# Selections ahead of the sliding part, early output norms, ten half-sequence tiles, and pair sums on VectorE

## The chip, the cores and the metric

The kernel runs on one core of a Trainium2 chip. The metric is the device time of one launch in microseconds (us); where several runs are told of, their median is meant. Engines are called PE (TensorE), DVE (VectorE), ACT (ScalarE), POOL (GpSimd) and SP (SyncE, which issues DMAs).

## The reference, cut to what matters

The program is one inference step of one decoder layer, for one prompt of 512 tokens and for eight sample sequences of 4 new tokens with 2048 past tokens each. Both share the weights and go through the same steps:

```
h = rmsnorm(x);  P = h @ W_in
x += W_out [ headnorm(NSA(P)) || sigmoid(o) * headnorm(mLSTM(P)) ]
x += CrossAttn(rmsnorm(x), memory);  x += SwiGLU(rmsnorm(x))
```

NSA is an attention in three branches per key-value group g (two groups). The compressed branch attends to 127 compressed blocks per sequence; they come from `compress`, run once for keys and once for values:

```
first = ch @ w1[:half];  second = ch @ w1[half:]      # ch: 16 tokens of one head side by side
hid = first + shift(second) + (pe @ w1 + b1);  out = gelu(hid) @ w2
```

The selected branch scores 64-token blocks by the compressed branch's probabilities, keeps the best 16, and attends to their raw rows:

```
imp = cmp_to_sel(p_c.sum(2));  imp = where(forced, 1e9, imp)
_, idx = top_k(imp, 16);       k_sel = gather(ks, idx); v_sel = gather(vs, idx)
```

The third branch is a sliding window of 512 tokens. Each head's output is then normalised.

## The kernel before

Products in fp32 are made of three matmuls in a reduced fp32 format: `split` (L212) writes a high part on ACT (L213) and the rest on DVE or POOL (L214), and `mm3` (L216) issues high by high, high by low, low by high (L218 to L220 in the trace).

The stages follow one another: the input projection, the prompt's attention and mLSTM, `compress(0)` for the keys, `compress(1)` for the values, the output projection w_out, cross attention, the feed-forward part. `weave` (L315) puts two streams of work into one program: `compress` is the background and pays 0.6 per yield, and the foreground (L1812) is the chain of prompt work, mLSTM of the samples, and `sample()`, whose yields cost 0.8 each. A scheduler that holds a time model of the engines then settles each engine's queue, and every engine works its queue in order.

`compress` walks over 8 sequences of 4 steps. `produce`, two steps ahead, transposes a tile (`xf`, DVE, L1191), splits it into `xh` (ACT) and `xl` (DVE), and forms the pair sum `xs` (POOL, L1198). `xf` has two buffers; `xh`, `xl` and `xs` have three. PE then runs 12 matmuls with `xh` and `xl` (L218 to L220) and a fp32 product of `xs` (L1296) per step.

`sample()` (L1417) does the sliding window for both groups, then the selected branch in a loop over g. For one g this loop reads the compressed keys (L1527), makes the softmax (L1605 to L1617), picks the blocks with top-k (L1624 to L1639), turns the pick into a mask `M4` (POOL), transposes key tiles (L1517) and scores them in four chunks ("quads", L1527), makes the softmax (L1672), and multiplies with the values (L1693). Keys and values come in half-sequence tiles called `gat`, 8 buffers, fetched by POOL with indirect DMAs (`half`, L1586). `finals_p` (L1391) adds the compressed branch to the prompt output and normalises it: squares (L1402), head sums by PE (L1407), Ln on ACT out of PSUM (L1408), Exp (L1413) and the scaling on DVE (L1414). It runs after g=0 of the selected loop. When `compress(1)` is through, `sample()` is drained (L1846), and the output projection follows in an order the scheduler chooses: chunks 0 and 1 of w_out on one half of the tokens (96 matmuls, here "group 1"), then chunks 2 and 3 ("group 2"). A chunk is fetched into `wraw` (L1830) and split by ACT (`whi`) and DVE (`wlo`); its products take `mh` and `ml`, the split prompt output.

## Time and profile before

| what | value |
|---|---|
| median of 3 runs | 1249.11 us (1246.6 to 1251.46) |
| the profiled execution | 1244.16 us, its span 1242.4 us |
| mean granted PE clock | 0.972 of full speed |
| PE, DVE, ACT, POOL busy | 95%, 67%, 50%, 45% of the span |

Matmuls are pipelined, so that a busy PE may still wait inside; where PE has no work the trace tells for each wait which instruction ended it. The granted clock of a stretch is a share of 2.4 GHz; 0.5 is the lower level of 1.2 GHz.

### The profile page before, as it was taken

The numbers are of one execution on the slowest core, as the hardware profiler recorded it, in microseconds if no ns is written. First come the engines' busy times: TensorE is split into PE (matmuls) and PEld (weight loads), VectorE is DVE, ScalarE is ACT, GpSimd is POOL, SyncE is SP. The second block draws the span as 40 slices with busy tenths as digits, with TensorE's granted clock in tenths as the row PEclk, the third lists the DMA queues.
The fourth block names the chain that finished last, engine by engine and source line by source line (L and its number), as shares of the span: only waits on it lengthen the run. The fifth ranks groups of instructions, "written<-read, shape, count | busy, mean of one in ns | idle before, by whom it ended". The sixth has DMA issues, their size and how long they took to land.

```text
span 1242.4 us, 24591 instructions
## 1 busy us (share of the span) xinstructions
PE 1174.2 (95%) x9220; PEld 1066.4 (86%) x9220; DVE 830.3 (67%) x1901; ACT 615.7 (50%) x1418; POOL 564.0 (45%) x686
## 2 busy tenths in 40 slices
PE   7999999899997989988899998999999999999996
PEld 5998999588885879846699977599899999999996
DVE  6336683567887787544566575544987887878874
ACT  5235665745646434474543233433575565565452
POOL 1013353566766366442243100034796586486442
PEclk9998999989997989998899999999999999999998
DMA  7324240141253184585468399650023322322411
GB/s 232 102 53 104 86 152 1 53 135 43 74 175 115 57 294 152 176 276 154 122 168 179 111 221 278 233 169 2 1 100 105 103 94 96 118 94 77 137 52 73
DMA packets 141769, 154.30 MB, mean 124 GB/s; under 512 B 17449, under 2 KB 123689, under 8 KB 141394
## 3 DMA queue, kind: packets, MB, share of 16 engines
q1 hardware_dynamic: 131922, 119.17, 32.1%
q0 software_dynamic: 9728, 33.56, 8.3%
q8 instruction: 73, 1.20, 0.4%
q14 instruction: 46, 0.38, 0.1%
HBM read 141.67 MB, written 13.12 MB: 125 GB/s over the span
## 4 chain that ended last, share of the span: by engine, by line
PE 53%; DVE 7%; DMA 5%; ACT 2%; issue 1%; POOL 1%; SPq 1%; POOLq 0%; DVEq 0%; ACTq 0%
PE xc L2260 7%; PE xa L2260 7%; PE bd L2260 6%; PE tp L2260 5%; PE bd L218 3%; PE bd L220 3%; PE bd L219 3%; PE xa L1296 2%; DMA wraw<-in_w_out 2%; DMA mkv<-in_cache_mem_k 2%; PE tp L1517 1%; PE bd L2159 1%; PE xc L218 1%; PE xc L219 1%; PE xc L220 1%
## 5 line engine op out<-in xcount | busy, mean ns | idle before, releaser
L214 POOL TENSOR_TENSOR al<-fraw,ah 128x512 fp32r<-128x512 f32 (+1 forms) x104 | 127.1, 1224 | 146.8 <-ACT ah L213 118.9
L213 ACT ACTIVATE whi<-wraw 128x1024 fp32r<-128x1024 f32 (+3 forms) x74 | 63.0, 890 | 70.1 <-DMA wraw<-in_w_xv 28.4
L214 DVE TENSOR_TENSOR wlo<-wraw,whi 128x1024 fp32r<-128x1024 f32 (+3 forms) x74 | 75.0, 1041 | 31.2 <-ACT whi L213 31.0
L213 ACT ACTIVATE ah<-fraw 128x512 fp32r<-128x512 f32 (+1 forms) x112 | 66.0, 594 | 43.8 <-PE xc L2260 11.8
L218 PE MATMUL bd<-w1h,xh 128*128 128x256 f32 x256 | 82.9, 326 | 0.0
L1198 POOL TENSOR_TENSOR xs<-xf 128x256 f32<-128x256 f32 x64 | 57.3, 902 | 48.5 <-PE xa L1296 29.7
L220 PE MATMUL bd<-w1h,xl 128*128 128x256 f32 x256 | 75.7, 298 | 1.4 <-DVE xl L214 1.4
L219 PE MATMUL bd<-w1l,xh 128*128 128x256 f32 x256 | 76.1, 298 | 0.0
L1296 PE MATMUL xa<-ws,xs 128*128 128x256 f32 x256 | 70.9, 399 | 1.9 <-DVE bq L1469 1.0
L625 POOL TENSOR_SCALAR sb<-sb,rs,gat 128x128 f32<-128x128 f32 (+3 forms) x64 | 46.2, 726 | 56.0 <-DVE rs L624 41.9
L213 ACT ACTIVATE xh<-xf 128x512 fp32r<-128x512 f32 x64 | 40.1, 632 | 43.6 <-DVE xf L1191 19.8
L213 ACT ACTIVATE ah<-sp 128x512 fp32r<-128x512 f32 (+1 forms) x64 | 35.6, 557 | 41.6 <-DVE sp L2200 16.9
L1191 DVE STREAM_TRANSPOSE xf<-cgat 128x512 f32<-128x512 f32 x64 | 44.9, 704 | 15.8 <-POOL xs L1198 15.0
L220 PEld LDWEIGHTS bd<-w1h,xl 128*128 128x128 f32 x256 | 49.1, 192 | 5.4 <-DVE xl L214 2.8
L219 PEld LDWEIGHTS bd<-w1l,xh 128*128 128x128 f32 x256 | 49.8, 195 | 4.3 <-issue 3.0
L214 DVE TENSOR_TENSOR xl<-xf,xh 128x512 fp32r<-128x512 f32 x64 | 48.2, 757 | 7.2 <-ACT xh L213 6.7
L1296 PEld LDWEIGHTS xa<-ws,xs 128*128 128x128 f32 x256 | 45.8, 198 | 8.1 <-issue 3.0
L218 PEld LDWEIGHTS bd<-w1h,xh 128*128 128x128 f32 x256 | 49.5, 195 | 3.7 <-issue 2.2
L219 PE MATMUL bd<-hlo,whi 128*128 128x272 f32 x176 | 52.4, 298 | 0.0
L218 PE MATMUL bd<-hhi,whi 128*128 128x272 f32 x176 | 52.2, 297 | 0.0
L220 PE MATMUL bd<-hhi,wlo 128*128 128x272 f32 x176 | 51.9, 295 | 0.0
L1874 POOL TENSOR_TENSOR acc<-acc,sq 128x272 f32<-128x272 f32 x35 | 31.4, 896 | 34.3 <-ACT sq L1873 33.9
(988 smaller groups left out, 4672.6 us busy)
## 6 DMA issues: line engine op xcount, KB each, us to landing
fraw<-in_w_gate SPq DMA_DIRECT2D x11, 1024.0 KB
fraw<-in_w_up SPq DMA_DIRECT2D x11, 1024.0 KB
fraw<-in_w_down SPq DMA_DIRECT2D x24, 384.0 KB
mkv<-in_cache_mem_k SPq DMA_DIRECT2D x64, 128.0 KB
mkv<-in_cache_mem_v SPq DMA_DIRECT2D x16, 512.0 KB
wraw<-in_w_in SPq DMA_DIRECT2D x8, 512.0 KB
wraw<-in_w_xq SPq DMA_DIRECT2D x4, 1024.0 KB
wraw<-in_w_xk SPq DMA_DIRECT2D x4, 1024.0 KB
```

The lines of the kernel that those rows point to most:

```text
L213: nc.scalar.activation(hi, src, AF.Copy)
L214: (eng or nc.gpsimd).tensor_tensor(lo, src, hi, op=OP.subtract)
L218: nc.tensor.matmul(out, ah, bh, start=first, stop=False, **kw)
L219: nc.tensor.matmul(out, ah, bl, start=False, stop=False, **kw)
L220: nc.tensor.matmul(out, al, bh, start=False, stop=last, **kw)
L625: (nc.vector, nc.gpsimd)[1].tensor_scalar(sb[:, :n], sb[:, :n], rs, gat[:, i, 3 * h + 1 + br:3 * h + 2 + br], op0=OP.mult, op1=OP.mult)
L1191: nc.vector.transpose(xf.rearrange("p a (q i) -> p q a i", q=4), gs[0].rearrange("p (q t a i) -> p t q a i", q=4, t=4, a=4)[:, t])
L1198: nc.gpsimd.tensor_tensor(xs_.rearrange("p c (v j) -> p v c j", v=2), xg[:, 0], xg[:, 1], op=OP.add)
L1296: nc.tensor.matmul(dst[2], ops[2][:, kk], w1s[t][2][:, kk], start=t == 0 and kk == 0, stop=t == 3 and kk == 1, skip_group_check=True)
L1517: nc.tensor.transpose(p[:, 128 * i:128 * i + 128], srcs(i), ident)
L1874: nc.gpsimd.tensor_tensor(acc[hf], acc[hf], sq, op=OP.add)
L2260: nc.tensor.matmul(p[:, :HALF], w[a][:, k], x[b_][:, k], start=first and k == 0 and i == 0, stop=last and k == n - 1 and i == 2, skip_grou ...
```

## The change

1. The pair sum `xs` moves from POOL to DVE and, in the text, ahead of the split.
2. The selection of group g becomes a generator `select(g)` that is called ahead of the sliding window of group g; the selected loop only reads its mask `sel[g]`.
3. `finals_p` is called ahead of the selected loop, and its four Ln and four Exp over 512 columns become four plain copies, one Ln and one Exp over 2048 columns.
4. `gat` gets ten buffers instead of eight; the second halves of the keys are fetched four at once, and the first key tiles of g=1 two after value chunk 0 and two after chunk 2, instead of four after chunk 2.

```
@@ produce
+                xs_ = cw.tile([128, 2, 128], F32, name="xs", bufs=3)
+                xg = xf.rearrange("p (v c) (g j) -> p g v c j", v=2, g=2)
+                nc.vector.tensor_tensor(xs_.rearrange("p c (v j) -> p v c j", v=2), xg[:, 0], xg[:, 1], op=OP.add)
                 xh, xl = [cw.tile([128, 2, 2, 128], R32, name=f"x{c}", bufs=3) for c in "hl"]
...
-                nc.gpsimd.tensor_tensor(xs_.rearrange("p c (v j) -> p v c j", v=2), xg[:, 0], xg[:, 1], op=OP.add)
@@ finals_p
-                    nc.scalar.activation(vj, p, AF.Ln, bias=eps_t)
+                    nc.scalar.activation(vj, p, AF.Copy)
...
+            nc.scalar.activation(var, var, AF.Ln, bias=eps_t)
+            nc.scalar.activation(var, var, AF.Exp, scale=-0.5)
             for j in range(4):
-                tc.keep_in_program_order(nc.scalar.activation(vj, vj, AF.Exp, scale=-0.5))
@@ sample
+            def select(g):
...
+                sel[g] = mk
             for g in range(2):
+                yield from select(g)
...
             kg = half("cache_k_slc", 0, 0)
+            yield from finals_p(sc.tile([128, 2080], F32, name="SS"))
             for g in range(2):
-                kh = half("cache_k_slc", g, 1, range(3))
...
+                kh = half("cache_k_slc", g, 1)
...
+                    if c == 0 and g == 0:
+                        kg = half("cache_k_slc", 1, 0, range(2))
                     if c == 2 and g == 0:
-                        kg = half("cache_k_slc", 1, 0)
+                        kg += half("cache_k_slc", 1, 0, range(2, 4))
```

On PE, around the last matmul of `compress(1)` (the last L220 with `w1h`), the queue of before goes on with two key groups and a quad of g=0, and then with finals_p (L1398) and the softmax's transposes (L1517 of SS):

```order
L220 MATMUL bd<-w1h_5412,xl 128x256
L1517 MATMUL tp<-ident,gat 128x128 x8
L1527 MATMUL sp<-kt,Qn 32x512 x4
L1246 MATMUL xc<-w_5309,hid 127x64 x4
L1398 MATMUL sp<-PcT,vcP 64x512 x2
L1216 MATMUL xc<-ident,ys 128x128 x4
L1517 MATMUL tp<-ident,SS 128x128 x4
```

In the changed kernel's PE queue at the same place the key transposes and quads of g=0 are still to come (its L1518 and L1528 are before's L1517 and L1527), and group 1 of w_out (L218 with `mh`) begins before the last of them:

```order
L220 MATMUL bd<-w1h_5412,xl 128x256
L1518 MATMUL tp<-ident,gat 128x128 x8
L1246 MATMUL xc<-w_5309,hid 127x64 x4
L1518 MATMUL tp<-ident,gat 128x128 x8
L1216 MATMUL xc<-ident,ys 128x128 x4
L1528 MATMUL sp<-kt,Qn 32x512 x4
L1518 MATMUL tp<-ident,gat 128x128 x16
L1528 MATMUL sp<-kt,Qn 32x512 x4
L1518 MATMUL tp<-ident,gat 128x128 x4
L1246 MATMUL xc<-w_5309,hid 127x64 x4
L1518 MATMUL tp<-ident,gat 128x128 x12
L1528 MATMUL sp<-kt,Qn 32x512 x4
```

Before, 56 of the 64 key transposes and three of the four quads of g=0 stood ahead of that last matmul; now 4 transposes and no quad do, so 52 transposes and three quads moved behind it. finals_p and the selection of g=1 went the other way, to places inside `compress(1)`. Further on, all 96 matmuls of group 1 now stand ahead of the values of g=0, and the PE queue of g=1 holds no w_out matmul between its keys (L1518), quads (L1528) and values (L1705):

```order
L1705 MATMUL po<-gat,PTs 32x128 x16
L1718 MATMUL po<-kvs,PN 128x128
L1518 MATMUL tp<-ident,gat 128x128 x16
L1528 MATMUL sp<-kt,Qn 32x512 x4
L1518 MATMUL tp<-ident,gat 128x128 x16
L1528 MATMUL sp<-kt,Qn 32x512 x4
L1518 MATMUL tp<-ident,gat 128x128 x16
L1528 MATMUL sp<-kt,Qn 32x512 x4
L1518 MATMUL tp<-ident,gat 128x128 x12
L1528 MATMUL sp<-kt,Qn 32x512 x4
```

Before, group 1 stood among the keys of g=1.

On ACT, the queue of before has four table loads in finals_p, and behind it the splits of w_out (`whi`) among the key copies `kt` of g=1; the exponentials of g=0 are long past there:

```order
L1408 ACT_TABLE_LOAD
L1408 ACTIVATE SS<-tp,eps_t 128x512 x2
L1607 ACT_TABLE_LOAD
L1607 ACTIVATE pcs,rs_6684<-pcs,nmn 128x127
L1408 ACT_TABLE_LOAD
...
L1413 ACT_TABLE_LOAD
...
L213 ACTIVATE whi<-wraw 128x1024
L206 ACTIVATE kt<-tp 128x512 x3
L213 ACTIVATE whi<-wraw 128x1024 x2
```

The changed kernel's ACT queue has two table loads; behind them the `kt` and the `whi` of chunks 0 and 1 come, and then the four `whi` of chunks 2 and 3 stand among the exponentials of g=0 (L1684, L1686) and the copies `PTs` that feed its values:

```order
L1411 ACT_TABLE_LOAD
...
L1412 ACT_TABLE_LOAD
...
L213 ACTIVATE mh<-oF 128x272 x8
...
L213 ACTIVATE whi<-cgat 128x1024 x2
L213 ACTIVATE whi<-wraw 128x1024
L206 ACTIVATE kt<-tp 128x512 x3
L213 ACTIVATE whi<-wraw 128x1024
L1686 ACTIVATE SS,bs_6536<-sn,nmn 128x32
L213 ACTIVATE whi<-wraw 128x1024
L1684 ACTIVATE SS,bs_6536<-SS,bs_6536 128x512 x4
L206 ACTIVATE PTs<-tp 128x512
L213 ACTIVATE whi<-wraw 128x1024
```

So the exponentials of g=0, which stood ahead of all splits of w_out, now stand behind both splits of chunk 2, and its last `PTs` behind a split of chunk 3.

## Rows read from the trace of the kernel before

**Rows 1.** The page: busy time of each engine, the chain that ended last by engine, and three groups of the costliest instructions (line, engine, operation, out<-in, count | busy us, mean ns | idle time before them and what ended it).

```profile
PE 1174.2 (95%) x9220; PEld 1066.4 (86%) x9220; DVE 830.3 (67%) x1901; ACT 615.7 (50%) x1418; POOL 564.0 (45%) x686
...
PE 53%; DVE 7%; DMA 5%; ACT 2%; issue 1%; POOL 1%; SPq 1%; POOLq 0%; DVEq 0%; ACTq 0%
...
L1198 POOL TENSOR_TENSOR xs<-xf 128x256 f32<-128x256 f32 x64 | 57.3, 902 | 48.5 <-PE xa L1296 29.7
...
L1191 DVE STREAM_TRANSPOSE xf<-cgat 128x512 f32<-128x512 f32 x64 | 44.9, 704 | 15.8 <-POOL xs L1198 15.0
```

**Rows 2.** Busy time of each engine in stretches of the span (from:to, length, then busy us and instructions of PE, PEld, DVE, ACT and POOL, the granted PE clock, DMA share, GB/s). Both compressions' steady part is 260 to 530; what follows up to 610 is the end of `sample()`.

```profile
260.00:530.00 270.00, 256.95 (x1929) 222.89 (x1928) 198.51 (x503) 134.12 (x341) 161.78 (x193) 0.96 0.43 134
380.00:400.00 20.00, 13.99 (x85) 10.68 (x83) 15.18 (x28) 13.22 (x31) 12.76 (x11) 0.66 0.38 120
440.00:460.00 20.00, 16.35 (x122) 14.34 (x120) 16.40 (x59) 7.11 (x14) 12.18 (x21) 0.83 0.94 324
460.00:530.00 70.00, 70.00 (x566) 60.60 (x565) 47.88 (x113) 30.98 (x64) 39.89 (x46) 1.00 0.53 166
530.00:550.00 20.00, 18.52 (x200) 10.24 (x199) 9.25 (x23) 13.68 (x30) 6.85 (x8) 1.00 0.80 272
550.00:570.00 20.00, 13.56 (x62) 6.93 (x62) 12.97 (x32) 16.87 (x28) 7.39 (x9) 0.74 0.45 153
570.00:590.00 20.00, 18.19 (x135) 15.97 (x134) 5.06 (x8) 5.15 (x8) 5.11 (x8) 0.91 0.75 228
590.00:610.00 20.00, 14.81 (x188) 9.91 (x188) 8.61 (x27) 10.96 (x26) 3.40 (x4) 0.83 0.18 57
```

**Rows 3.** PE from 529 to 613 in order of time (start us, us, instruction, count, idle time before it and what ended it): the last matmul of `compress(1)`, a quad, a part of finals_p, the first quads of g=1, four key transposes, and the first matmul of group 2.

```profile
530.07 0.28 PE L220 MATMUL bd<-w1h,xl 128*128 128x256 f32 x1
...
532.23 1.06 PE L1527 MATMUL sp<-kt,Qn 128*32 128x512 f32 x8 [1.00 <-ACT kt L206]
...
544.64 1.07 PE L1398 MATMUL sp<-PcT,vcP 32*64 32x512 f32 x4
...
546.65 1.12 PE L1407 MATMUL tp<-SS,bones 128*128 128x512 f32 x2
...
566.16 1.91 PE L1527 MATMUL sp<-kt,Qn 128*32 128x512 f32 x2
568.01 0.66 PE L1517 MATMUL tp<-ident,gat 128*128 128x128 f32 x4
...
610.50 0.37 PE L218 MATMUL xa<-mh,whi 128*128 128x272 f32 x1
```

**Rows 4.** What two of the engines waited for, summed (us, times, longest us): PE from 440 to 560, POOL and DVE from 260 to 530.

```profile
PE xc L1216 <- DVE vcP L1268: 2.4, 1, 2.4
PE xa L1296 <- DVE bq L1469: 1.0, 1, 1.0
...
POOL xs L1198 <- PE xa L1296: 29.7, 15, 4.6
...
DVE xf L1191 <- POOL xs L1198: 15.0, 15, 2.5
```

**Rows 5.** Durations (ns, least, median, greatest; first and last start; form) of the subtraction `xl` over 512 columns and of a DVE addition of the pair sum's shape.

```profile
L214 DVE TENSOR_TENSOR xl<-xf,xh x64: 649/684/1609, 252.0 to 517.7; 128x512 fp32r<-128x512 f32 x64
...
L1332 DVE TENSOR_TENSOR ys<-xa,cur x16: 379/415/426, 273.6 to 529.9; 128x256 f32<-128x256 f32 x16
```

**Rows 6.** ACT in order of time, from 546 on: table loads, the Ln and Exp of finals_p, splits of `mh`, and the split of w_out chunks 2 (578, 582) and 3 (589).

```profile
547.13 1.28 ACT L1408 ACT_TABLE_LOAD   x1
548.42 0.69 ACT L1408 ACTIVATE SS<-tp,eps_t 128x512 f32<-128x512 f32 x1
...
554.86 1.38 ACT L213 ACTIVATE mh<-oF 128x272 fp32r<-128x272 f32 x4
...
560.17 0.62 ACT L1413 ACTIVATE SS<-SS 128x512 f32<-128x512 f32 x1
560.70 0.58 ACT L206 ACTIVATE kt<-tp 128x512 f32<-128x512 f32 x1
...
578.28 1.06 ACT L213 ACTIVATE whi<-wraw 128x1024 fp32r<-128x1024 f32 x1 [4.91 <-DMA wraw<-in_w_out]
582.54 1.06 ACT L213 ACTIVATE whi<-wraw 128x1024 fp32r<-128x1024 f32 x1 [3.19 <-DMA wraw<-in_w_out]
...
589.62 1.06 ACT L213 ACTIVATE whi<-wraw 128x1024 fp32r<-128x1024 f32 x1 [1.30 <-DMA wraw<-in_w_out]
```

**Rows 7.** DVE in order of time from 530 to 573: the scaling at the end of finals_p, and the last `wlo` of w_out chunk 1.

```profile
558.78 2.79 DVE L1414 SCALAR_TENSOR_TENSOR oF<-oF,gh,SS 128x512 f32<-128x512 f32 x4 [2.06 <-ACT SS L1413]
...
567.65 1.21 DVE L214 TENSOR_TENSOR wlo<-wraw,whi 128x1024 fp32r<-128x1024 f32 x1
```

**Rows 8.** SP's issues of w_out chunks 2 and 3, then, from the chain that ended last between 525 and 615, the last quad of g=1 (start us, us, what).

```profile
568.89 1.28 SPq L1830 DMA_DIRECT2D wraw<-in_w_out  x2
...
584.88 1.25 SPq L1830 DMA_DIRECT2D wraw<-in_w_out  x2
...
594.38 1.14 PE sp L1527 x8
```

**Rows 9.** POOL in order of time from 536 to 592: the first gather of g=1's key tiles, with the wait ahead of it, and the last of the eight.

```profile
543.19 0.94 POOL L573 DMA_INDIRECT gat<-in_cache_k_slc,gx  x1 [9.95 <-PE po L1693]
...
552.94 0.94 POOL L573 DMA_INDIRECT gat<-in_cache_k_slc,gx  x1 [0.30 <-issue]
```

More of the change, by code (lines that the diff above doesn't have):

```diff
@@ L1503, in load_win @@
             def load_win(nm, b):
-                t_ = sc.tile([128, 2, 4, 128], F32, name="gat", bufs=8)
+                t_ = sc.tile([128, 2, 4, 128], F32, name="gat", bufs=10)
                 nc.sync.dma_start(t_, I[nm][0, b:b + 2].rearrange("b (p a) v d -> p b a (v d)", a=4))
@@ L1588, in half @@
                 for q in qs:
-                    t_ = cgs["free"].pop(0) if ex else sc.tile([128, 1024], F32, name="gat", bufs=8)
+                    t_ = cgs["free"].pop(0) if ex else sc.tile([128, 1024], F32, name="gat", bufs=10)
                     gather(t_, name, 4 * g + q, 1 + hf)
@@ L1598, in sample @@
                 nmn = sc.tile([128, 12], F32, name="nmn", bufs=2)
-                kh = half("cache_k_slc", g, 1, range(3))
-                yield from need(("c", 0))
-                pc = bank(psp)
-                quad(pc[:, 0:127], bs, lambda q: kcT[:, bs[q], 0:127])
-                pcs = sc.tile([128, 128], F32, name="pcs")
-                nc.vector.memset(pcs[:, 127:128], 0.0)
-                nc.vector.tensor_tensor_reduce(pcs[:, 0:127], pc[:, 0:127], K0, 1.0, BIG, op0=OP.add, op1=OP.min,
-                                               accum_out=nmn[:, 0:1])
-                nc.scalar.activation(pcs[:, 0:127], pcs[:, 0:127], AF.Exp, scale=-1.0, bias=nmn[:, 0:1],
-                                     accum_out=rs[:, 0:1])
-                nc.vector.reciprocal(rs[:, 3:4], rs[:, 0:1])
-                nc.vector.tensor_scalar(pcs[:, 0:127], pcs[:, 0:127], rs[:, 3:4], None, op0=OP.mult)
-                blk = sc.tile([128, 32], F32, name="blk")
-                edge = sc.tile([128, 32], F32, name="edge")
-                p4 = pcs.rearrange("p (j r) -> p j r", r=4)
-                nc.vector.tensor_reduce(blk, p4[:, :, 0:3], axis=AX.X, op=OP.add)
-                nc.vector.tensor_copy(edge, p4[:, :, 3])
-                nc.vector.tensor_tensor(edge[:, 1:32], edge[:, 1:32], p4[:, 0:31, 3], op=OP.add)
-                nc.vector.scalar_tensor_tensor(blk, edge, 0.5, blk, op0=OP.mult, op1=OP.add)
+                kh = half("cache_k_slc", g, 1)
                 yield
@@ L1643, in sample @@
                                             B0[:, i].rearrange("p (j r) -> p j r", r=4),
-                                            mk[:, :, None].to_broadcast([128, 32, 4]), op=OP.add)
-                kh += half("cache_k_slc", g, 1, (3,))
+                                            sel[g][:, :, None].to_broadcast([128, 32, 4]), op=OP.add)
                 yield
@@ L1708, in sample @@
                 yield
-                if g == 0:
-                    yield from finals_p(sc.tile([128, 2080], F32, name="SS"))
             pop("sc")
```

60 lines of the change are left out of this document (41 added, 19 removed).

## The prediction, written before the changed kernel ran

> **What bounds the kernel now.** I read the page first: PE is busy for 95% of the span and holds 53% of the chain that ended last, no other engine more than 7% [rows 1]. So a change counts by what it does to PE's work and to its holes. The windows show where the holes are. In the steady part of the two compressions PE is busy for 256.95 of 270 us, and the last 70 us of it are full [rows 2]. The hole at 380 to 400 (6.0 us) belongs to the loading of the value weights, which the change does not touch. The one at 440 to 460 (3.65 us) is where `sample()` begins: PE waits 2.4 us for `vcP` and 1.0 us for `bq`, both late on DVE [rows 4]. Behind the last compression matmul it is worse: from 530 to 610 PE is busy for 18.52 + 13.56 + 18.19 + 14.81 = 65.1 of 80 us, in part at a granted clock of 0.74 [rows 2]. I call that last matmul's start C (530.07) and the first matmul of group 2 of w_out D (610.50) [rows 3]; behind D the program is the same in both kernels. The time moves by what happens to C, and by what happens to the stretch from C to D, 80.4 us before.
>
> **Pair sums.** POOL loses 64 instructions, 57.3 us [rows 1], that are not on the chain. DVE gains 64. Its price is not in the trace of before; a DVE addition of the same shape with two inputs took 415 ns at the median, and `xl`, which has twice the columns, 684 ns [rows 5]. The bounds are 64 x 0.415 = 26.6 us and 64 x 0.684 = 43.8 us; I take the row of the same shape. DVE is busy for 198.5 of 270 us there [rows 2], so it becomes 225 us, 83%. PE covers that as long as `xl` comes in time. The waits matter more. `xs` may start only when PE has read the `xs` three steps back, and POOL waited 29.7 us for this, 15 times, 4.6 us at most [rows 4]. That wait moves onto DVE, an in-order queue, with `xl`, the compression's own `ys` and the foreground's small operations behind it. DVE is no stranger to it: `xf` waited 15.0 us, also 15 times, for `xs` on POOL [rows 4], since it has two buffers. So DVE waits 29.7 instead of 15.0 us at most, 14.7 us more. PE has two steps in hand, and 270 us for some 64 steps make 4.2 us a step, so 8.4 us of cover against a longest wait of 4.6. I put it at 0; if the cover is gone, at up to +14.7. On the other side lies the hole at 440, where DVE's queue is not shorter but POOL's is; it can give back 3.4 us at most, and I take 0.5.
>
> The trace has one more sign: `xl` takes 649 ns at least and 1609 at most [rows 5], so DVE is now and then held up. The Trainium skill explains such a case (SBUF — State Buffer, "Who interferes with whom"): a VectorE instruction with two SBUF inputs and a GpSimd instruction that reads SBUF exclude each other, and the later one waits the earlier one out. Here the rule speaks both ways, for the new `xs` on DVE has two SBUF inputs and meets what POOL still does, while `xl` no longer meets `xs` on POOL; its bad end is one of the rivals below.
>
> **Work across C.** Ahead of C the program loses 52 key transposes, that is 13 groups of four at 0.66 us or a little less where they overlap (I take 0.59, which gives 7.7 us), and three quads at 1.06 us, 3.2 us [rows 3]. It gains finals_p's products: four times 1.07 us (L1398) and four times 0.56 us (L1407, 1.12 for two), 6.5 us, and the selection of g=1, whose three small products I estimate at 1.1 us from the quad's row. PE was full there, so C comes 10.9 - 7.6 = 3.3 us earlier. The clock is 1.00 [rows 2] and I see no reason for it to fall there.
>
> **From C to D.** Counted from C, with rows of before.
> - finals_p ends in ACT: two loads of 1.28 us, and a Ln and an Exp over 2048 columns. From 0.69 and 0.62 us over 512 [rows 6] these cost between 1.3 us (half the columns' price, a guess at what fixed cost is saved) and 2.8 us (four times); I take 1.9. That makes 2.6 + 3.8 = 6.4 us; before, the same part ran from 547.13 to 560.79, 13.7 us [rows 6].
> - The scaling's first quarter follows (0.7 of 2.79 us [rows 7]), then eight `mh` (2.8), two `kt` (1.1), four `whi` of 1.06 us and a last `wlo` of 1.2 us [rows 6, 7]: w_out chunk 2 can be asked for at C + 17 to 18.5, where before it was C + 38.8 (568.89 [rows 8]).
> - In before its second half was ready 13.65 us after the issue (568.89 to 582.54 [rows 6, 8]). So its last `whi` is done at C + 33.2. The exponentials of g=0 are behind it on ACT, though its quads are through by about C + 22 (52 transposes, four quads and the copies). That is a new wait of some 9 to 11 us. Group 1, 96 matmuls, covers part of it on PE.
> - Exponentials and `PTs` take 3.3 us more, the last `PTs` waits for chunk 3, 4.7 us from issue to `whi` (584.88 to 589.62 [rows 6, 8]), and the values of g=0 end at about C + 43.
> - The third and fourth key tiles of g=1 wait for buffers that value chunk 1 of g=0 gives back (before, the first gather had waited 9.95 us for a value product too [rows 9]). They land at about C + 46. Four chunks of keys and quads at about 4.5 us each (transposes 0.66 x 4 and copies, ACT and DVE sharing them) bring the last quad to C + 64. In before the last quad began at 594.38 and D came at 610.50 [rows 3, 8], 16.1 us, less the quad's own 1.1. That gives C + 64 + 15 = C + 79.
>
> So C to D is 79 us against 80.4. Its lower end, without the hold of 9 to 11 us, is 69. Its upper end is 87: g=1 now runs without dense work between its pieces, and before, with the same lack of cover, quads took 1.91 instead of 1.06 us at the lower clock [rows 3]; 0.85 us for each of four quads and about as much for each chunk's transposes and the values make 8 us.
>
> **The sum.** -0.5 (hole at 440), -3.3 (C), -1.4 (C to D) = -5.2 us, against the profiled execution of 1244.16 us: 1238.9 us. That execution lies 4.95 us under the median of 1249.11, so I forecast 1243.9, say 1244 us. The ends of the terms together: -3.4 - 3.3 - 11.4 = -18.1 us and 0 - 3.3 + 6.6 + 14.7 = +18.0 us.
>
> **The rivals.**
> - No hold. The chunk 2 load comes in time, since it is issued some 20 us earlier and fewer gathers run beside it. C to D is 69 us, the sum -0.5 - 3.3 - 11.4 = -15.2, the time 1234. For it: DMA share is 0.75 in 570 to 590 and 0.45 in 550 to 570 [rows 2], so the load was slowed by neighbours. Against it: the two halves still took 13.65 us, and ACT's order is fixed.
> - Uncovered g=1. Group 1 is used up ahead of the values of g=0; g=1 runs at the low clock, C to D is 87. The sum is -3.8 + 6.6 = +2.8, the time 1252. For it: 590 to 610, where no w_out work was left, had PE at 14.81 of 20 us and a clock of 0.83 [rows 2]. Against it: 16 transposes per chunk keep PE rather busy.
> - DVE's queue is the bound (the other side): `xs` stops the queue ahead of `xl` and `ys`, and PE stands. It decides when DVE's waits in the steady part, 15.0 us in before, grow by more than PE's two steps can hide, 8.4 us at a time. With half to all of the 14.7 us on PE, and the other terms as forecast, the sum is +2 to +9.5; with the last rival as well, +10 to +17. I price it at +10, 1259. The skill's rule would add to it: if each of 64 `xs` lost what the longest `xl` lost (1609 - 684 = 925 ns), DVE would have 198.5 + 26.6 + 59.2 = 284 us of work in 270 us. The median of `xl`, 684 against a least of 649, says that such meetings are rare.
> - The change moves work but the scheduler's order gives it all back, C to D grows by as much as C shrinks: 1249.
>
> **How the numbers follow.** Forecast (1239 to 1248) 0.36; no hold 0.22; uncovered g=1 (1249 to 1256) 0.18; DVE's queue 0.16; all given back 0.08. A measurement of this kernel can tell some 0.5%, 6.2 us, from no change. Faster by more: no hold 0.22, 0.16 of the forecast's 0.36 (its part below 1242.9), together 0.38. Slower by more (above 1255.4): 0.15 of DVE's queue and 0.07 of uncovered g=1 (its upper end, where a part of DVE's waits comes on top), 0.22. The rest, 0.40, is within. The range reaches from 1231 to 1261, and leaves 0.2 out; the likeliest case alone has 1239 to 1248.
>
> **What would show it.** In the changed profile, `xs` on DVE at about 0.42 us and DVE's wait for L1296 near 29.7 us, with no new waits of PE for `xl` or `xh` between 260 and 525; the last L220 with `w1h` at 526 to 527; two table loads and about 6.4 us for Ln and Exp; a wait of ACT for `wraw` ahead of the exponentials of g=0, about 10 us; group 2 of w_out about 79 us behind C. It is wrong if PE waits for `xl`, `xh` or `xs` by several us before C, if C to D is under 72 or over 85 us, or if anything behind D changes its length by more than 2 us.

## The result and the profile after

The changed kernel takes 1257.58 us at the median of 6 runs (1255.62 to 1260.66), the kernel before 1247.51 us over 6 runs on the same chip. The ratio is 1.008, with a 95% interval of 1.0056 to 1.0104: it is slower by some 10 us, where 1244 us and a gain were forecast. The profiled execution of the changed kernel has a span of 1258.2 us against 1242.4, so the two profiles lie further apart than the medians.

In PE's order of time, C (the last compression matmul) and D (the first matmul of group 2) are these lines of the changed kernel's trace (columns as in [rows 3]):

```profile
536.30 0.28 PE L220 MATMUL bd<-w1h,xl 128*128 128x256 f32 x1
...
592.48 1.06 PE L1528 MATMUL sp<-kt,Qn 128*32 128x512 f32 x8 [0.35 <-issue]
...
608.38 1.06 PE L1528 MATMUL sp<-kt,Qn 128*32 128x512 f32 x8 [0.69 <-ACT kt L206]
...
621.65 0.37 PE L218 MATMUL xa<-mh,whi 128*128 128x272 f32 x1
```

C is 6.2 us later than in [rows 3] instead of 3.3 earlier, and C to D is 85.35 us instead of 80.43. From D to the end it is 636.6 us against 631.9, more than the 2 us that the prediction allowed. Over the 18 other profiles below this last stretch is 630.7 to 639.3 us and goes with no edit; I take it as spread. So what has to be explained lies ahead of D.

The windows of the changed kernel that answer to [rows 2] (same columns):

```profile
260.00:530.00 270.00, 249.91 (x1838) 213.69 (x1836) 205.03 (x567) 131.11 (x333) 105.12 (x128) 0.93 0.41 129
380.00:400.00 20.00, 12.59 (x75) 9.23 (x75) 10.58 (x34) 12.73 (x33) 11.06 (x11) 0.50 0.34 107
440.00:460.00 20.00, 14.97 (x103) 12.68 (x103) 13.26 (x55) 5.42 (x11) 6.12 (x6) 0.74 0.93 343
460.00:530.00 70.00, 68.25 (x528) 58.01 (x526) 52.34 (x147) 31.79 (x65) 23.94 (x26) 1.00 0.45 143
```

PE is busy for 7 us less between 260 and 530, and the granted clock falls from 0.96 to 0.93 there. The clock falls at two places, 380 to 400 and 440 to 460. DVE is not what is full: 205 of 270 us, where I had forecast 225.

The first place is the seam between the two compressions, by which I mean the time between the last matmul of the first with its split weights (`w1h`, `w1l`) and the first such matmul of the second. Here is the trace of before, DVE, POOL and SP in order of time (L1041 makes `wvz`, a small product of the mLSTM state; L1045 is its consumer on DVE; L1168 transposes the prompt's columns `pp`; L588 loads the compression's weights, `r` the last of them):

```profile
382.72 1.64 POOL L1041 TENSOR_TENSOR wvz<-vms,wN 32x512 f32<-32x512 f32 x1
383.79 0.69 DVE L1168 STREAM_TRANSPOSE pp<-r 128x512 f32<-128x512 f32 x1
385.95 1.18 POOL L573 DMA_INDIRECT cgat<-in_cache_v_cmp,gx  x1 [0.31 <-DVE xf L1191]
387.00 5.78 SPq L588 DMA_DIRECT2D r<-in_cmp_w_v  x2
...
388.71 0.70 DVE L1045 TENSOR_TENSOR W<-wvz,W 32x512 fp32r<-32x512 f32 x1
```

And the changed kernel at the same place:

```profile
381.72 1.89 POOL L573 DMA_INDIRECT cgat<-in_cache_v_cmp,gx  x1 [6.39 <-DVE xf L1191]
383.92 0.95 POOL L573 DMA_INDIRECT cgat<-in_cache_v_cmp,gx  x1 [0.30 <-issue]
385.17 0.95 POOL L573 DMA_INDIRECT cgat<-in_cache_v_cmp,gx  x1 [0.30 <-DVE csm L1379]
386.42 0.95 POOL L573 DMA_INDIRECT cgat<-in_cache_v_cmp,gx  x1 [0.30 <-DMA wr<-in_cmp_w_v]
387.39 1.05 POOL L1041 TENSOR_TENSOR wvz<-vms,wN 32x512 f32<-32x512 f32 x1
...
389.13 0.68 DVE L1045 TENSOR_TENSOR W<-wvz,W 32x512 fp32r<-32x512 f32 x1 [4.19 <-ACT W L1043]
389.82 0.71 DVE L1168 STREAM_TRANSPOSE pp<-r 128x512 f32<-128x512 f32 x1
390.56 1.11 SPq L588 DMA_DIRECT2D r<-in_cmp_w_v  x2
```

Read it upwards from the last line. SP asks for the weights `r` at 390.56 because they overwrite the columns that `pp` reads. `pp` stands on DVE behind L1045, which waits 4.19 us. L1045 waits (through ACT) for `wvz` on POOL, and `wvz` stands behind four gathers, the first of which has itself waited 6.39 us for a transpose on DVE. In before `wvz` is ahead of these four gathers and `pp` ahead of L1045. What changed is the order of two queues that are worked in order. The seam, in which PE works on other products but on none of these matmuls, reaches from 374.17 to 405.75, where before it was from 380.14 to 390.59. How much of this longer seam the wait for `r` accounts for is a question for e6 below.

What that does to PE's clock is in the windows of the two traces, before first and the changed kernel in the next fence (the columns as above: PE busy first, granted clock third from the end):

```profile
375.00:390.00 15.00, 8.96 (x72) 7.23 (x71) 13.48 (x32) 10.17 (x21) 13.26 (x13) 0.79 0.45 139
390.00:405.00 15.00, 12.94 (x69) 10.45 (x60) 9.43 (x18) 8.51 (x23) 6.39 (x6) 0.64 0.27 90
```

```profile
375.00:390.00 15.00, 4.32 (x29) 2.85 (x30) 10.76 (x31) 5.66 (x12) 7.67 (x9) 0.60 0.52 161
390.00:405.00 15.00, 14.38 (x67) 10.39 (x66) 9.31 (x25) 11.90 (x31) 3.72 (x4) 0.50 0.10 31
```

PE had little to do until 390, and the 14.4 us of work after that ran at the lower level, 1.2 GHz.

Behind C, ACT of the changed kernel shows the two table loads, the wide Ln and Exp, and the hold:

```profile
537.09 1.28 ACT L1411 ACT_TABLE_LOAD   x1
538.38 2.00 ACT L1411 ACTIVATE SS<-SS,eps_t 128x2048 f32<-128x2048 f32 x1
...
542.18 1.91 ACT L1412 ACTIVATE SS<-SS 128x2048 f32<-128x2048 f32 x1
...
573.92 1.06 ACT L213 ACTIVATE whi<-wraw 128x1024 fp32r<-128x1024 f32 x1 [10.09 <-DMA wraw<-in_w_out]
...
576.13 0.71 ACT L1684 ACTIVATE SS<-SS,bs 128x512 f32<-128x512 f32 x1
```

The wide exponentials of g=0 do stand behind the splits of w_out, with a wait of 10.09 us, and begin at C + 39.8 instead of the forecast C + 33.2.

### The profile page after: what moved, and what is told of

Same layout as the page of the kernel before. It is cut to its first block, busy times and chain, and to the rows that moved or that the text cites. A ratio compares the mean times of both kernels' runs of the same rounds, so it can differ in the third digit from the quotient of the medians.

```text
span 1258.2 us, 24511 instructions
## 1 busy us (share of the span) xinstructions
PE 1174.7 (93%) x9220; PEld 1066.2 (85%) x9220; DVE 845.9 (67%) x1965; ACT 613.9 (49%) x1414; POOL 508.9 (40%) x622
## 3 DMA queue, kind: packets, MB, share of 16 engines
q1 hardware_dynamic: 131922, 119.17, 31.6%
## 4 chain that ended last, share of the span: by engine, by line
PE 75%; DVE 9%; DMA 7%; ACT 4%; issue 2%; SPq 1%; POOL 1%; another core or an unknown queue 0%; POOLq 0%; DVEq 0%; ACTq 0%
PE xc L2272 7%; PE xa L2272 7%; PE bd L218 7%; PE bd L220 7%; PE bd L219 7%; PE bd L2272 5%; PE tp L2272 5%; PE xa L1296 4%; PE tp L1518 2%; DMA wraw<-in_w_xv 1%; PE xc L219 1%; PE tp L634 1%; PE xc L218 1%; PE xa L218 1%; PE xc L220 1%
## 5 line engine op out<-in xcount | busy, mean ns | idle before, releaser
L218 PE MATMUL bd<-w1h,xh 128*128 128x256 f32 x256 | 80.3, 315 | 0.6 <-ACT hidt L1329 0.6
L220 PE MATMUL bd<-w1h,xl 128*128 128x256 f32 x256 | 75.5, 299 | 0.3 <-DVE xl L214 0.2
L1296 PE MATMUL xa<-ws,xs 128*128 128x256 f32 x256 | 71.0, 407 | 3.0 <-DVE xs L1195 1.5
L219 PE MATMUL bd<-w1l,xh 128*128 128x256 f32 x256 | 73.5, 288 | 0.0
L213 ACT ACTIVATE xh<-xf 128x512 fp32r<-128x512 f32 x64 | 40.3, 632 | 56.9 <-DVE xf L1191 22.3
L573 POOL DMA_INDIRECT cgat<-in_cache_v_cmp,gx x32 | 32.8, 1026 | 72.4 <-DVE dns L1075 25.9
L1296 PEld LDWEIGHTS xa<-ws,xs 128*128 128x128 f32 x256 | 47.7, 203 | 11.5 <-issue 3.5
L218 PEld LDWEIGHTS bd<-w1h,xh 128*128 128x128 f32 x256 | 48.5, 190 | 6.0 <-issue 2.7
L218 PE MATMUL bd<-hhi,whi 128*128 128x272 f32 x176 | 51.8, 294 | 0.0
L220 PEld LDWEIGHTS bd<-w1h,xl 128*128 128x128 f32 x256 | 48.2, 190 | 4.2 <-issue 2.0
L220 PE MATMUL bd<-hhi,wlo 128*128 128x272 f32 x176 | 51.5, 293 | 0.0
L573 POOL DMA_INDIRECT cgat<-in_cache_k_cmp,gx x32 | 33.8, 1057 | 38.7 <-DVE xf L1191 11.7
L214 DVE TENSOR_TENSOR xl<-xf,xh 128x512 fp32r<-128x512 f32 x64 | 44.5, 700 | 6.5 <-ACT xh L213 3.8
L214 DVE TENSOR_TENSOR al<-sp,ah 128x512 fp32r<-128x512 f32 (+1 forms) x64 | 40.7, 636 | 9.6 <-ACT ah L213 7.6
```

What stands on the lines that cost most here:

```text
L213: nc.scalar.activation(hi, src, AF.Copy)
L214: (eng or nc.gpsimd).tensor_tensor(lo, src, hi, op=OP.subtract)
L218: nc.tensor.matmul(out, ah, bh, start=first, stop=False, **kw)
L219: nc.tensor.matmul(out, ah, bl, start=False, stop=False, **kw)
L220: nc.tensor.matmul(out, al, bh, start=False, stop=last, **kw)
L573: nc.gpsimd.indirect_dma_start(out=dst, out_offset=None, in_=I[name][0].rearrange("n (c t) v d -> (n c) (t v d)", t=t), in_offset=bass.Ind ...
```

## The experiments

Theory A: C is late because of `xs` on DVE, at the seam. Theory B: C is late because finals_p and the selections run inside the second compression. For C to D: the hold on ACT that my schedule has, the want of tiles, or the late place of the sliding windows. The table gives each run's ratio to the kernel before on its chip with its interval, and from its one profile C, C to D and the first quad of g=0 against C (all in us; minus is ahead of C).

| run | edit | ratio (95%) | C | C to D | first quad |
|---|---|---|---|---|---|
| before | | 1 | 530.1 | 80.4 | -23.4 |
| changed | all four edits | 1.0080 (1.0056 to 1.0104) | 536.3 | 85.4 | +9.1 |
| e1 | before, xs on DVE | 1.0079 (1.0055 to 1.0103) | 536.2 | 84.2 | -18.8 |
| e2 | changed, xs on POOL | 1.0079 (1.0051 to 1.0106) | 528.2 | 90.5 | +8.1 |
| e3 | changed, finals_p back | 1.0018 (0.9994 to 1.0043) | 529.7 | 81.0 | -2.1 |
| e4 | before, selections ahead | 1.0059 (1.0036 to 1.0082) | 527.4 | 90.5 | -5.7 |
| e5 | changed, xs on DVE for values only | 0.9972 (0.9948 to 0.9997) | 525.0 | 78.9 | +5.7 |
| e6 | e1, wvz on DVE | 0.9945 (0.9915 to 0.9975) | 522.7 | 73.3 | -23.9 |
| e7 | changed, short yields | 1.0059 (1.0036 to 1.0082) | 534.2 | 83.8 | +9.1 |
| e8 | e4, short yields | 0.9979 (0.9952 to 1.0007) | 526.3 | 82.7 | -3.6 |
| e9 | changed, wvz on DVE | 1.0049 (1.0028 to 1.0071) | 521.4 | 96.8 | +19.0 |
| e10 | before, wvz on DVE | 1.0046 (1.0016 to 1.0075) | 527.6 | 89.1 | -22.3 |
| e11 | e6, ten tiles | 0.9971 (0.9942 to 1.0000) | 526.7 | 74.7 | -22.6 |
| e12 | e3, wvz on DVE | 0.9989 (0.9969 to 1.0009) | 523.4 | 85.3 | +1.4 |
| e13 | changed, no hold | 1.0074 (1.0050 to 1.0099) | 535.7 | 88.1 | +9.1 |
| e14 | changed, selections behind | 1.0027 (1.0008 to 1.0045) | 535.5 | 75.7 | -2.1 |
| e15 | e14, e9 and e13 together | 1.0031 (1.0010 to 1.0053) | 536.0 | 79.4 | +1.1 |
| e16 | e6 with e13 | 0.9972 (0.9947 to 0.9998) | 533.8 | 75.5 | -24.4 |
| e17 | e6 again | 0.9975 (0.9959 to 0.9991) | 532.5 | 74.3 | -22.1 |
| e18 | e5 and e14 together | 1.0027 (1.0009 to 1.0044) | 532.4 | 77.2 | +4.6 |

**e1, xs alone.** The kernel before with edit 1 of the diff.

```
+                nc.vector.tensor_tensor(xs_.rearrange("p c (v j) -> p v c j", v=2), xg[:, 0], xg[:, 1], op=OP.add)
-                nc.gpsimd.tensor_tensor(xs_.rearrange("p c (v j) -> p v c j", v=2), xg[:, 0], xg[:, 1], op=OP.add)
```

> The kernel before with edit 1 alone: the pair sum xs on DVE, ahead of the split. Theory A (the last compression matmul comes 6 us later because xs on DVE changes the pace of the two compressions and their seams near 380 and 440): that matmul at 533 to 537 instead of 530.1, DVE waiting for L1296, and 1250 to 1256 us. Theory B (it comes later because finals_p and the selections now run inside the second compression): that matmul at 528 to 531 and 1244 to 1249 us, no slower than before.

It is as slow as the whole change, and C is where the change has it. In its trace the seam is long again, 29.4 us against 31.6 in the changed kernel and 10.5 before; SP's wait for `pp` is 7.0 us here and 7.7 us there, and none of before's waits of SP at the seam is for `pp`. Here is that wait, e1's line:

```profile
SPq L588 <- DVE pp L1168: 7.0, 1, 7.0
```

Theory A holds for C. Theory B is out: e1 has finals_p and the selections at their old place.

**e2, everything but xs.** The changed kernel with edit 1 undone: `xs` is on POOL again, behind the split.

> The changed kernel with xs back on POOL behind the split. Theory A: the last compression matmul at 527 to 531, the stretch from it to group 2 of w_out still 83 to 87 us, 1249 to 1253 us. Theory B: that matmul still at 535 to 537, 1256 to 1259 us.

C is at 528.2, as theory A has it, 1.8 us ahead of before. But the time is as long as the changed kernel's, where theory A had 1249 to 1253 us: C to D is 90.5 us instead of 83 to 87, and D to the end, 639.3, is the longest of all profiles. So edits 2 to 4 cost some 0.8% by themselves, behind C; they and edit 1 do not add up.

**e3, finals_p back.** The changed kernel with finals_p at its old place and in its old form (edit 3 undone).

> The changed kernel with finals_p back behind g=0 and with its four Ln and four Exp. Theory on the tail (ACT's order, the exponentials of g=0 behind the splits of w_out chunk 2, comes from finals_p being done early): the hold goes, the stretch from the last compression matmul to group 2 of w_out is 72 to 81 us, 1247 to 1253 us. Rival (the order comes from the keys of g=0 being late, whatever finals_p does): the stretch is still 83 to 88 us and ACT still waits some 10 us for w_out ahead of these exponentials; 1255 to 1260 us.

The stretch is 81.0 and the time within 0.5% of before. ACT's exponentials of g=0 stand ahead of the splits of w_out again. Undoing edit 3 takes back about 0.6% of the 0.8%. The first quad of g=0 is 11 us earlier against C, and the seam is as long as in e1 (29.4 us).

**e4, selections alone, and e8, their yields counted at 0.01.** e4 is before with edit 2; e8 differs from e4 by

```
             def select(g):
...
-                yield
+                yield 0.01
```

> The kernel before with edit 2 alone: the selections ahead of the sliding windows. If the selections cost nothing where they now run and take top-k's chain out of the end: the last compression matmul at 530 to 532 (some 1 us of products comes in ahead of it) and the stretch behind it 76 to 80 us, 1243 to 1249 us. If they push the key transposes of g=0 behind that matmul by themselves: it is at 526 to 529, the stretch 82 to 87 us, 1248 to 1253 us.

> e4 (before with the selections moved ahead) with their yields counted at 0.01. Credit theory: the first quads of g=0 come at about 20 us ahead of the last compression matmul, as in before, and not at -5.7; the matmul at 529 to 532, the stretch behind it 78 to 83 us, 1243 to 1248 us. Rival (the selection's work itself, or its place, turns the end's order over): the stretch stays at 87 to 91 us, 1250 to 1255 us.

The second line of e4's expectation has its C (527.4) and its time (1252.95 us, 1.0059), but a shorter stretch than the 90.5 us found. In e4 the sliding windows end late. The trace tells this by the last value product of the windows, one line each for before, the changed kernel and e4 (least, median, greatest duration, first and last start):

```profile
L1578 PE MATMUL po<-gat,PTs x64: 272/273/297, 473.5 to 497.8; 128*32 128x128 f32 x64
```

```profile
L1625 PE MATMUL po<-gat,PTs x64: 270/273/297, 493.0 to 524.1; 128*32 128x128 f32 x64
```

```profile
L1624 PE MATMUL po<-gat,PTs x64: 272/273/297, 483.0 to 512.9; 128*32 128x128 f32 x64
```

15 us later by the selections alone, 26 us with the whole change. The tiles of the windows are the tiles of the keys of g=0 (`gat`), so the keys come later and have less of the compression to run under. With the yields made short (e8) the stretch is 82.7 and the loss is gone, 0.9979. The long yields thus cost the time, but not in the way that the credit theory has it: the windows still end late, at 513.8, and the first quad lies 3.6 us ahead of C, not 20 and less than e4's 5.7. Late windows alone do not make the stretch long: e3 and e5 have their last such product at 519.1 and 513.8, and stretches of 81.0 and 78.9 us.

**e5, xs on DVE in the second compression only.** The seam is built of what stands on DVE and POOL at the end of the first one.

```
-                nc.vector.tensor_tensor(xs_.rearrange("p c (v j) -> p v c j", v=2), xg[:, 0], xg[:, 1], op=OP.add)
+                (nc.vector if kv else nc.gpsimd).tensor_tensor(xs_.rearrange("p c (v j) -> p v c j", v=2), xg[:, 0], xg[:, 1], op=OP.add)
```

> The changed kernel with xs on DVE for compress(1) only (POOL does it for compress(0), both ahead of the split). Seam theory (xs on DVE costs at the seam between the two compressions: POOL's gathers move ahead of wvz, DVE waits for it with the prompt columns behind, and the value weights come late): the seam without compression matmuls is 10 to 13 us instead of 31.6, the last compression matmul at 527 to 531 as in e2. Rival (DVE's longer queue slows both compressions throughout): the seam may shrink, but that matmul stays at 533 to 537. The stretch behind it is the scheduler's and may be 82 to 91 us in either; 1250 to 1257 us by the first, 1255 to 1261 us by the second.

The seam is 12.3 us and C at 525.0, earlier than the 527 to 531 expected: what makes the seam long is `xs` on DVE in the first compression, and half of the `xs` on DVE cost the second nothing that shows. The stretch fell as well, to 78.9, below the 82 to 91 expected, and the kernel is faster than before by 0.3% (3.8 us), with an interval that just leaves out 1. This is nearly what was forecast for the whole change: a C that is a few us earlier, 79 us from C to D, and 5.2 us won. But e2, with the same edits 2 to 4, has a stretch of 90.5, so the order that e5 got there may be luck.

**e6, e1 with wvz on DVE, e10, wvz alone on before, and e9, on the changed kernel.**

```
-            nc.gpsimd.tensor_tensor(wvz, vms[:, :, 0:128], wN[:, 0:4, None].to_broadcast([32, 4, 128]), op=OP.mult)
+            nc.vector.tensor_tensor(wvz, vms[:, :, 0:128], wN[:, 0:4, None].to_broadcast([32, 4, 128]), op=OP.mult)
```

> e1 (before with xs on DVE) and wvz (L1041) moved from POOL to DVE, so that it no longer stands behind POOL's four gathers at the seam. Seam theory: DVE's 4.2 us wait ahead of the prompt columns goes, the r weights are asked for 3 to 8 us earlier than 393.9, the seam is 20 to 26 us instead of 29.4, the last compression matmul at 530 to 534, 1248 to 1254 us. Rival (the seam is set elsewhere, by ACT or the weights' own loads): seam 28 us or more, that matmul at 535 to 537, 1254 to 1260 us.

> The kernel before with wvz on DVE alone, xs on POOL. Seam theory: before, wvz stood ahead of POOL's gathers anyway and the prompt columns ahead of its consumer, so there is no wait to take away: the last compression matmul at 527 to 531, same time, 1240 to 1247 us (ratio 0.997 to 1.003). Rival (e6's gain is wvz's own, whatever xs does): matmul at 521 to 525 and a ratio of 0.993 to 0.996.

> The changed kernel with wvz on DVE as in e6. If the seam is where edit 1 costs in the full change too: the r weights are asked for at 383 to 387 instead of 390.6, the last compression matmul at 527 to 531 instead of 536.3; the stretch behind it stays at 80 to 86 us, since the sliding windows stay late (their last value product within 15 us of that matmul); 1245 to 1251 us. Rival (what e6 gained was an accident of the order): that matmul at 534 to 538, 1254 us or more.

In e6's trace `wvz` no longer waits for the gathers, and L1045 follows without a wait:

```profile
382.45 0.94 POOL L573 DMA_INDIRECT cgat<-in_cache_v_cmp,gx  x1 [0.30 <-issue]
382.60 0.62 DVE L1041 TENSOR_TENSOR wvz<-vms,wN 32x512 f32<-32x512 f32 x1
...
384.10 0.68 DVE L1045 TENSOR_TENSOR W<-wvz,W 32x512 fp32r<-32x512 f32 x1
384.80 0.71 DVE L1168 STREAM_TRANSPOSE pp<-r 128x512 f32<-128x512 f32 x1
...
385.54 1.11 SPq L588 DMA_DIRECT2D r<-in_cmp_w_v  x2
```

Counted from the last matmul of the first compression, `r` is asked for after 12.8 us in e6 (372.70 to 385.54) and 16.4 us in e1 (377.55 to 393.94): the wait was real, and without it `r` is asked for 3.6 us sooner. e9 shows the same 12.8 us against 16.4 in the changed kernel.

The seam, however, did not shrink to the 20 to 26 us of the seam theory: it is 28.4 us in e6 against 29.4 in e1, which the rival had, and 28.3 in e9. So the wait for `pp` and `r` is not what ends it. The first of these matmuls in the second compression needs the first split `w1h<-wr`, and ACT makes it late. Here is ACT in before, in the changed kernel and in e6 (L1107 makes `kz` for the mLSTM):

```profile
388.42 1.06 ACT L213 ACTIVATE w1h<-wr 128x1024 fp32r<-128x1024 f32 x1 [0.98 <-DMA wr<-in_cmp_w_v]
389.38 4.77 ACT L1107 ACTIVATE kz<-K,bm 96x128 fp32r<-96x128 f32 x16
```

```profile
393.87 4.78 ACT L1107 ACTIVATE kz<-K,bm 96x128 fp32r<-96x128 f32 x16
398.56 1.99 ACT L213 ACTIVATE w1h<-wr 128x1024 fp32r<-128x1024 f32 x2
```

```profile
391.71 4.77 ACT L1107 ACTIVATE kz<-K,bm 96x128 fp32r<-96x128 f32 x16
...
396.91 1.99 ACT L213 ACTIVATE w1h<-wr 128x1024 fp32r<-128x1024 f32 x2
```

In before the first split follows its load and `kz` comes after it; in the two others the splits stand behind `kz` and wait for no load. Counted from the last matmul of the first compression they begin after 8.3 us in before, 24.4 in the changed kernel and 24.2 in e6. In all 13 profiles with `xs` on DVE in both compressions this is 24.2 to 24.4 us and the seam 28.3 to 32.3 us; in the other seven the split comes after 7.0 to 9.0 us and the seam is 10.4 to 14.6 us. So in those 13 the seam has to be over 24 us whenever `r` is asked for; behind the first split PE works off other products for another 7.2 us in the changed kernel, from 398.56 to 405.75. Edit 1 makes the seam long, then, by the order of ACT's and PE's queues too. No run moves the splits alone, so what they are worth is not shown.

The times say more than the seam: e6 is 0.55% faster than before, where e1 was 0.8% slower. By its profile it gained 11 us against e1 in the stretch behind C, which the edit does not touch, and e9 lost 11 there against the changed kernel. Their C of 522.7 and 521.4 are earlier than the 530 to 534 and the 527 to 531 that I gave them; e17 below shows how little a single C is worth. e10, where there was nothing to mend, is slower than before by the stretch alone (89.1). So the stretch is turned over by edits that have no business in it; I take it that the scheduler chooses its order from the time at which its model reaches it.

**e7, short yields in the changed kernel.** As e8, in select and in finals_p.

> The changed kernel, with the yields of select and of finals_p counted at 0.01 instead of 0.8, so that they no longer let the compression run ahead of the keys of g=0. Credit theory (the keys fell behind the last compression matmul because the moved parts' yields stand ahead of them): two or more quads of g=0 lie ahead of that matmul again, it comes at 537 to 541, the stretch behind it is 74 to 80 us, 1248 to 1254 us. Rival (the scheduler puts them there for want of buffers or engines): the quads stay behind it, the stretch 83 to 87 us, 1255 to 1260 us.

The quads stay at +9.1, which is the rival's side. The ratio is 1.0059 instead of 1.0080, and the two intervals overlap, so a gain is not shown.

**e11, ten tiles on e6, and e12, finals_p back with wvz on DVE.**

> e6 (before with xs and wvz on DVE) and edit 4: ten half-sequence tiles and the earlier fetches of g=1's keys. If tiles are short at the end (in before, POOL waited 9.95 us for a buffer ahead of the first gather for g=1): the keys of g=1 come earlier, the stretch behind the last compression matmul is 68 to 73 us against 73.3, ratio to before 0.990 to 0.995. Rival (the order, not the buffers, sets the stretch, and it is turned over again): 74 to 84 us, ratio 0.995 to 1.003.

> e3 (the changed kernel with finals_p at its old place and in its old form) and wvz on DVE. Seam theory: the r weights are asked for 5 to 8 us earlier, the last compression matmul at 521 to 526 instead of 529.7, the stretch behind it 78 to 84 us, ratio to before 0.993 to 0.999. Rival: no earlier matmul, ratio 1.000 to 1.005.

e11's stretch is 74.7, no better than e6's: a gain from edit 4 is not shown. e12 has C at 523.4 as the seam theory has it, though its seam is 32.1 us, and a stretch of 85.3, beyond what I gave it; together no difference to before.

**e13, the hold taken away.** Issue order alone: the splits of chunks 2 and 3 are queued behind the last `PTs` copy of g=0 on ACT (`hot["ex"]` is that copy).

```
...
-                wk[c] = wo_chunk(c)()
+                with tc.issue_after(hot["ex"].ins):
+                    wk[c] = wo_chunk(c)()
```

> The changed kernel with the splits of w_out chunks 2 and 3 queued on ACT behind the last PTs copy of g=0 (issue order alone, no wait added). Hold theory: ACT's 10.1 us wait for w_out ahead of the exponentials goes, the values of g=0 end 8 to 10 us earlier, and the stretch behind the last compression matmul is 75 to 79 us instead of 85.3; 1248 to 1253 us, ratio to before 1.000 to 1.004. Rival (group 1 of w_out fills PE meanwhile and g=1 is bound by its keys' tiles): the stretch is 82 to 86 us, ratio 1.005 to 1.010.

The wide exponentials of g=0 begin at 568.35 instead of 576.13, and D is no earlier. What was won is lost in g=1, as two quads, two windows and a split of chunk 3 of this run show:

```profile
593.72 1.93 PE L1529 MATMUL sp<-kt,Qn 128*32 128x512 f32 x8 [2.24 <-ACT kt L207]
...
600.41 1.94 PE L1529 MATMUL sp<-kt,Qn 128*32 128x512 f32 x8
```

```profile
575.00:595.00 20.00, 13.20 (x157) 7.67 (x154) 6.73 (x10) 6.91 (x10) 11.97 (x12) 0.94 0.84 255
595.00:624.00 29.00, 24.75 (x222) 14.59 (x219) 10.29 (x35) 12.14 (x28) 1.53 (x3) 0.69 0.20 79
```

```profile
597.77 1.06 ACT L214 ACTIVATE whi<-wraw 128x1024 fp32r<-128x1024 f32 x1 [1.51 <-DMA wraw<-in_w_out]
```

Two of four quads of g=1 take 1.9 instead of 1.06 us, at a clock of 0.69 in these 29 us (0.94 from 595 to 622 in the changed kernel). Ahead of that PE had been busy for 13.2 of 20 us, against 14.93 in the changed kernel from 575 to 595, with no product of w_out in either; that this is the reason for the lower clock is my inference. The hold is real, but taking it away won nothing (1.0074 against 1.0080): it is the theory that falls.

**e14, the selections behind the windows.**

```
             for g in range(2):
-                yield from select(g)
...
             kg = half("cache_k_slc", 0, 0)
+            for g in range(2):
+                yield from select(g)
```

> The changed kernel with both selections behind the sliding windows, ahead of finals_p. Theory (the selections make the windows late, so that key tiles come free late): the last value product of the windows at 505 to 512 instead of 524, one quad or more of g=0 ahead of the last compression matmul, that matmul at 536 to 540, the stretch behind it 74 to 81 us; ratio 1.001 to 1.005. Rival (xs and finals_p make them late): that product at 518 to 526, the stretch 83 us or more, ratio 1.006 to 1.010.

The windows end at 498.9, nearly as in before (497.8); a quad of g=0 is ahead of C, and the stretch is 75.7. The place of the selections made the windows late, and with it the stretch was long in the changed kernel; by e3 and e5 the late windows are not enough for that. What is left of the loss (1.0027) is, by this profile, C at 535.5.

**e15, e16, e18: the causes together.**

> The changed kernel with all three: wvz on DVE, the selections behind the windows, and the splits of chunks 2 and 3 behind PTs of g=0. If the three causes are independent: the last compression matmul at 521 to 527, the stretch 74 to 80 us, group 2 at 597 to 605, ratio to before 0.989 to 0.996. If each time only the scheduler's order is turned over: ratio 0.998 to 1.006.

> e6 (before with xs and wvz on DVE) with the splits of w_out chunks 2 and 3 behind the last PTs copy of g=0. In e6 the exponentials of g=0 already stood ahead of them, so the hold theory expects no change: the stretch 72 to 75 us, ratio to before 0.992 to 0.997. Another result says that the order behind C is turned over by anything.

> The changed kernel with xs on DVE for compress(1) only and the selections behind the sliding windows. If the two causes add: seam 10 to 13 us, the last compression matmul at 523 to 528, the windows' last value product at 488 to 498, the stretch behind that matmul 72 to 78 us, ratio to before 0.989 to 0.995. If only the order is turned over again: ratio 0.996 to 1.004.

**e17, e6 again.**

> e6 once more (before with xs and wvz on DVE), in more rounds. If the gain is real: ratio to before 0.993 to 0.998, with an interval that leaves out 1. If e6 was a lucky draw of the clock: 0.997 to 1.002. Its profile: the seam 28 to 32 us, the last compression matmul anywhere from 522 to 534, earlier where the granted clock is back at full before 400.

e16 has e6's order instruction by instruction on PE, DVE, ACT and POOL, since there the splits stood behind anyway, and so has e17 by its making. Their ratios are 0.9945, 0.9972 and 0.9975, and 0.9975 has the narrowest interval: e6's order is faster than the changed kernel, and faster than before by 0.25% or a little more. Their profiles, however, have C at 522.7, 533.8 and 532.5. Part of the 10 to 11 us comes in and behind the seam, and there the granted clock tells the runs apart. These are two stretches of 15 us in e6, e16 and e17 in turn, the first from the last matmul of the first compression on:

```profile
372.70:387.70 15.00, 4.03 (x36) 2.74 (x35) 12.69 (x36) 5.51 (x12) 7.59 (x10) 0.62 0.58 171
387.70:402.70 15.00, 14.94 (x99) 11.03 (x97) 10.26 (x25) 12.43 (x32) 3.74 (x4) 0.81 0.14 46
```

```profile
374.24:389.24 15.00, 4.02 (x36) 2.74 (x35) 12.71 (x36) 5.51 (x12) 7.59 (x10) 0.57 0.56 171
389.24:404.24 15.00, 15.00 (x67) 11.37 (x65) 7.94 (x21) 11.80 (x29) 3.78 (x4) 0.52 0.11 41
```

```profile
377.22:392.22 15.00, 4.04 (x36) 2.74 (x35) 12.69 (x36) 5.50 (x12) 7.59 (x10) 0.59 0.55 172
392.22:407.22 15.00, 15.00 (x76) 11.34 (x73) 9.24 (x22) 11.80 (x29) 3.41 (x4) 0.61 0.10 37
```

The first stretch is the same in all three, 36 matmuls and 4.0 us of PE; in the next one PE does 99, 67 and 76 matmuls. The rest lies elsewhere: the first compression had ended 4.5 us earlier in e6 than in e17 (372.70 against 377.22), and from the seam's end to C e6 takes 121.7 us, e16 127.3 and e17 124.4. So one profile's C is good to some 10 us where the seam is long, and only the timed ratios decide. The stretch of these three is 73.3, 75.5 and 74.3 us, so it goes with the order; e16's stretch and ratio lie just outside what I gave them. e15 and e18 show that the mended causes do not add: both keep a short stretch, but C is at 536.0 and 532.4, and they are slower than before by 0.3%. The combination gave nothing that e5 or e6 alone did not give.

## Why the prediction was wrong

The forecast was 1244 us, faster than before; the measured 1257.58 us lies in the range of 1231 to 1261, on the other side of before.

- **Pair sums.** Wrong, and this is the step that failed first. "I put it at 0" rested on PE's two steps in hand against a longer DVE queue, and in that frame it was right: `xs` took 413 ns at the median (forecast 415), PE waited 0.7 us for it between 260 and 530, and DVE waited for L1296 only 7.2 us, not 29.7 (us in all, times, longest):

```profile
DVE xs L1195 <- PE xa L1296: 7.2, 5, 3.1
```

  The cost lay elsewhere. With `xs` gone from POOL to DVE the scheduler put the queues in another order at the seam between the compressions, of which the prediction said that the change does not touch it: `pp` and `wvz` fell behind a wait, ACT's splits of the value weights fell behind `kz`, and the seam grew from 10.5 us to 29.4 in e1. e1 says what edit 1 is worth: 0.8%, about 10 us, inside my bound of 14.7, by a mechanism that none of my rivals named. By its profile 6.1 us of it lie ahead of C and 3.8 behind. e5 ties the seam to `xs` in the first compression; which of the reorderings costs how much stays open. My rival on DVE's queue had one of the engines and the wrong place: it looked for `xl` and `ys` as what is queued behind, not for the seam. Of the rule of the Trainium skill on two SBUF inputs (SBUF — State Buffer, "Who interferes with whom") this trace shows no effect that counts: `xl`'s median is 680 ns in the changed kernel, 684 in [rows 5], and DVE's busy time rose by 6.5 us only.
- **The hole at 440.** I took -0.5; PE's busy time there went from 16.35 to 14.97 us of 20. The wait for `vcP` is 3.6 instead of 2.4 us [rows 4].
- **Work across C.** The sign was right and the size off, as far as one profile tells. e2, with `xs` on POOL, has C 1.8 us earlier, not 3.3 + 0.5. One term was mis-sized: the L1407 row of [rows 3] shows two instructions for one head pair, so four of them cost 4 x 1.12 = 4.5 us, not 2.2.
- **From C to D.** 79 forecast, 85.4 measured, inside the range of 69 to 87. The hold was there, 10.09 us (forecast 9 to 11), the table loads and the wide Ln and Exp cost 2 x 1.28 + 2.00 + 1.91 = 6.5 us (6.4), and the last quad came to D in 13.3 us (15). The step that failed is the one ahead of it, "w_out chunk 2 can be asked for at C + 17 to 18.5": it was asked for at C + 28 (564.28), since seven key copies `kt`, three of them with waits for PE's transposes, stood ahead of `mh` on ACT behind C and kept it back to 553.55. I had put two `kt` there. And the hold, which I counted as 9 to 11 us of the stretch, is worth nothing by e13: without it g=1 ran at the lower clock, as in my second rival. The row that I read there as a quad at the lower clock (1.91 us [rows 3]) is two of a quad's eight matmuls; e13's whole quads take 1.93 us, so the price was right all the same.
- **What I did not see.** The order shows where instructions stand, and I priced the 52 transposes that moved behind C by PE's time alone. Behind C each chunk can also be a wait for gathers, copies and softmax. e4, e14 and e3 show what moved them: the selections ahead of the windows (edit 2), finals_p with them (edit 3). But that their place alone makes the stretch long is not shown: e5 and e18 have no quad of g=0 ahead of C, and stretches of 78.9 and 77.2 us.
- **The sum.** The parts do not add: edit 1 alone 0.8%, edits 2 to 4 without it 0.8%, all four 0.8%. A better price for one term would not have given this.

What stays open: why the stretch from C to D is 73 us in e6 and 97 us in e9. Late windows, uncovered quads and the lower clock go with it in some runs (e4, e9, e13) and not in others; e10's 89 us, with its first quad as early as in before, is not explained by them, and no run holds the whole order fixed but for one of the changes. It also stays open which queue's order makes the seam long.
